# S5 scan over sixteen groups at a time, its matrices on VectorE alone, and the value projection moved ahead of queries and keys

## The chip, the cores and the metric

The kernel runs on one core of one Trainium2 chip. The metric is the device time of one execution in microseconds; below, the median of three executions is given, and beside it the time and the span of the one execution that was profiled. The engines are TensorE (PE), VectorE (DVE), ScalarE (ACT), GpSimd (POOL) and SyncE (SP), which here issues the transfers.

## The reference, cut to what matters

A two-layer trunk works on 1152 tokens of 1024 features (1024 latent tokens and 128 context tokens). The first layer runs neighbourhood attention and a bidirectional diagonal state-space model (S5) side by side on one input projection:

```
hp = h @ w_in
q, k, v, u = split(hp)             # 512 features each
q = rmsnorm(q); k = rmsnorm(k)
na = neighbourhood_attention(q, k, v)
# S5: 32 groups of 16 channels, 64 complex states, two directions
bu = B_bar u                       # per group
h[t] = A_bar * h[t-1] + bu[t]      # complex, forward and backward
y = gelu(D u + Re(C h))
y = y * sigmoid(y @ w_glu + b_glu)
out = concat(na, y) @ w_out
```

After it come a gated ConvFFN, a layer of grouped-query attention, and another ConvFFN. Nothing of those is touched here.

## The kernel before, in words

**The stage.** What matters lies in the first 510 us of some 3270. After the tables of S5 and the first part of the modulation are made, the 1152 tokens are normalised in six chunks of 192 (tiles `xc`, `n_t`, `n_rs`) and split into a high and a low part (`h0h` and `h0l`). A projection multiplies each by the split weights (`w_hi`, `w_lo`) in three products; DVE makes `h0l`, POOL makes `w_lo`. Then four blocks of `u` (tile `u_p`), eight blocks of queries and keys of three column chunks each (24 chunks; `qk_norm` takes the squares on ACT, a mean on PE into `ps_n`, two operations on `q_rs` and one on `qk_o` on DVE), and eighteen tiles of values (`v_o`). The accumulators `ps_b` have three buffers, so PE can be at most three chunks ahead of the operation that empties them.

**S5 setup.** `s5_setup` builds, for eight blocks of four groups each, input matrices (`s5tmp` into `s5win`, transposed on PE) and output matrices (`s5T`) with a product table (`s5tz`, many small matmuls). Of each block's twelve tensor operations six stood on DVE and six on POOL.

**S5 main.** `s5_main` handles the 32 groups in four parts of eight. `states` multiplies the inputs `s5U` by `s5win` on PE, ACT copies the result into `s5L`, and DVE scans it: time is cut in nine segments of sixteen steps, and all segments step at once, so that one step is four operations (two products `s5t`, two additions to `s5L`) on a strided slice; a short second scan (`s5hin`) joins the segments. `outputs` expands the segments' start states (`s5p`, four products of 128x512, and one sum), adds them to the scanned states (`s5hp`, two operations of 64x1016), multiplies on PE, stores `s5Y`, reloads it transposed (`s5yc`), applies gelu (`s5yo`) and stores it for the gate. In each block two of the four products and one of the two additions stood on POOL. `s5L` had two buffers, and the scan of one part was woven with the outputs of the part before.

**Order.** Instructions are placed on each engine's queue by a scheduler from the order of the program, the dependencies and the buffers; S5 is issued from within the projection's loops with high priority (`s5_on`). Every queue runs strictly in its order. After the stage, `mix` loads the four gelu results, the gate (`ygh`, `glu_ps`) needs all four, and the attention loads `na_q` and `na_k` from the stored queries and keys.

Of the kernel before, what the change touches and what calls it, by code (L numbers as in the profile page):

```python
# [29 lines left out]
BH = slice(64, 128)  # L30
# [130 lines left out]
def s5_setup(K, I, S, bp, P):  # L161
# [102 lines left out]
    for b in range(8):  # L264
        g = slice(4 * b, 4 * b + 4)
        d4 = lambda ap: ap.rearrange("p (g s c) -> p g s c", g=4, s=8)
        tmp = [d4(t) for t in half("X0") + half("X1")]
        vv = [d4(t) for t in half("X2")]
        e = (dve, pool)
        P4 = lambda t: [bc(x[:, g], (128, 4, 8, 16), 3) for x in t]  # L270
        C4 = lambda t: [bc(x[:, g], (128, 4, 8, 16), 2) for x in t]
        cmul(K, vv, P4(pv), C4(bb), tmp, e=e)
        win = bp.tile([128, 2, 4, 128], F32, tag="W", name="s5win")
        with K.tc.high_priority():
            for r in range(2):
# [33 lines left out]
        tz = bp.tile([128, 240], F32, tag="tz", name="s5tz")  # L309
        act.activation(tz, pz[:, :240], AF.Copy)  # L310
        K.stt(tz[:, 112:128], i16, dd[:, b : b + 1], pz[:, 112:128], ALU.mult, ALU.add)
        K.load(S.tz[4 * b : 4 * b + 4].rearrange("g c n -> (g c) n"), tz)
        yield


def s5_main(K, I, S, bp, P, yg):
# [2 lines left out]


    dve, act, pool = K.dve, K.act, K.pool
    G = 8

    def step(cur, prev, aR, aS, shape):
        x = ((1, 3), (3,)) if len(shape) == 4 else ((1,), ())
        for src, c in ((prev, bc(aR, shape, *x[0])), (prev[:, ::-1], bc(aS, shape, *x[1]))):
            t = bp.tile([128, 2, G, 9], F32, tag="t", name="s5t", bufs=2)
            if len(shape) == 3:
                t = t[:, :, :, 0]
            K.tt(t, src, c, ALU.mult)  # L330
            K.tt(cur, cur, t, ALU.add)

    def states(m, out):
        gs = slice(G * m, G * m + G)
        out.U = U = bp.tile([128, G, 144], F32, tag="U", name="s5U", bufs=2)
        K.load(U, S.ud[m].rearrange("s c g k -> (s c) g k"))
        out.L = L = bp.tile([128, 2, G, 144], F32, tag="L", name="s5L", bufs=2)
        out.hin = hin = bp.tile([128, 2, G, 8], F32, tag="hin", name="s5hin", bufs=2)
        for b2 in range(2):
            win = bp.tile([128, 2, 4, 128], F32, tag="W", name="s5win2", bufs=2)  # L340
            K.load(win.rearrange("p r g n -> p (r g n)"), S.win[2 * m + b2])
            for n0 in (0, 2):
                for r in range(2):
                    pt = P("s")
                    for j in range(2):
                        K.pe.matmul(pt[:, j * 144 : (j + 1) * 144], lhsT=win[:, r, n0 + j], rhs=U[:, 4 * b2 + n0 + j], start=True, stop=True)
                    src = pt[:, :288].rearrange("p (g n) -> p g n", n=144)
                    dst = L[:, r, 4 * b2 + n0 : 4 * b2 + n0 + 2]
                    act.activation(dst[FH], src[FH], AF.Copy)
                    act.activation(dst[BH, :, 0:128], src[BH, :, 127::-1], AF.Copy)  # L350
                    act.activation(dst[BH, :, 128:144], src[BH, :, 143:127:-1], AF.Copy)
                yield
        Lv = L.rearrange("p r g (s j) -> p r g s j", j=16)
        for j in range(1, 16):
            step(Lv[:, :, :, :, j], Lv[:, :, :, :, j - 1], S.a8R[:, gs], S.a8S[:, :, gs], (128, 2, G, 9))
            yield

        pool.tensor_copy(S.fin[:, :, gs], Lv[:, :, :, 8, 15])
        dve.tensor_copy(hin[:, :, :, 0], S.init[:, :, gs])
        for i in range(7):  # L360
            dve.tensor_copy(hin[:, :, :, i + 1], Lv[:, :, :, i, 15])
            step(hin[:, :, :, i + 1], hin[:, :, :, i], S.a128R[:, gs], S.a128S[:, :, gs], (128, 2, G))
        yield

    def outputs(m, q):
        wia = bp.tile([128, 8, 128], F32, tag="wia", name="s5wia")
        for s in range(8):
            K.load(wia[16 * s : 16 * s + 16], S.tz[8 * m : 8 * m + 8, 0:16, (7 - s) * 16 : (7 - s) * 16 + 128].rearrange("g c n -> c g n"))
        Y = bp.tile([128, G, 144], F32, tag="Y", name="s5Y")
        init = S.init[:, :, G * m : G * m + G]  # L370
        for b2 in range(2):
            lg = slice(4 * b2, 4 * b2 + 4)
            g = slice(G * m + 4 * b2, G * m + 4 * b2 + 4)
            wout = bp.tile([128, 2, 4, 128], F32, tag="V", name="s5wout")
            K.load(wout.rearrange("p r g n -> p (r g n)"), S.wout[2 * m + b2])
# [1 line left out]
            p = [bp.tile([128, 2, 4, 8, 16], F32, tag=f"P{i}", name=f"s5p{i}") for i in range(2)]  # L377
            for r in range(2):
                shp = (128, 4, 8, 16)
                K.tt(p[0][:, r], bc(q.hin[:, r, lg], shp, 3), bc(S.awR[:, g], shp, 2), ALU.mult)  # L380
# [4 lines left out]
            lb = q.L[:, :, lg]  # L385
# [9 lines left out]
            for n0, n1 in ((0, 2), (2, 4)):  # L395
                pt = P("s")
                for j in range(n0, n1):
                    K.acc(
                        pt[:, (j - n0) * 144 : (j - n0 + 1) * 144],
                        [(wia[:, b2 * 4 + j], q.U[:, b2 * 4 + j]), (wout[:, 0, j], hp[:, 0, j]), (wout[:, 1, j], hp[:, 1, j])],  # L400
                    )
                act.activation(Y[:, b2 * 4 + n0 : b2 * 4 + n1], pt[:, : (n1 - n0) * 144].rearrange("p (g n) -> p g n", n=144), AF.Copy)
            yield
# [10 lines left out]
    class Part:  # L414
        pass

    old = None
    for m in range(5):
        new = Part()
        todo = [states(m, new)] if m < 4 else []  # L420
        if old:
            todo.append(outputs(m - 1, old))
        while todo:
            for g in todo[:]:
                if next(g, g) is g:
                    todo.remove(g)
                else:
                    yield
        old = new

# [903 lines left out]
def tile_hybrid_step(ctx, tc, I, O):  # L1334
# [110 lines left out]
    for m in range(8):  # L1445
        u = W.get(I["w_qk"][m])
        for a, b in CH:
# [8 lines left out]
                K.load(O["na_k"][128 * (m - 4) : 128 * (m - 4) + 128], o[:, 256:384])  # L1456
            s5_on(3)
            next(parts, None)
    for hf in range(2):
        ws = [W.get(I["w_v0"][hf, kk]) for kk in range(2)]  # L1460
        for t in range(9):
            ps = P("b")
            token_major(K, ps[:, :256], ws, H, t)
            o = qp.tile([128, 384], F32, tag="qk", name="v_o", bufs=2)
            act.activation(o[:, :256], ps[:, :256], AF.Copy)
            K.load(S.vd[t][:, 256 * hf : 256 * hf + 256], o[:, :256])
            if t == 8:
                K.load(O["na_v"][:, 256 * hf : 256 * hf + 256], o[:, :256])
# [352 lines left out]
```

## Time and profile before

| quantity | value |
|---|---|
| median of 3 runs | 3267.01 us (3266.26 to 3275.08) |
| profiled execution: time, span | 3276.04 us, 3274.2 us |
| PE busy, share of the span | 2979.5 us, 91% |
| DVE busy | 1853.3 us, 57% |
| ACT busy | 1379.8 us, 42% |
| POOL busy | 1168.9 us, 36% |

The shares are averages over stages with different limits: over the whole span PE leads, but in the stage of this change other engines end the waits. A timeline row gives the start, the duration, the engine, the line, the operation, out<-in and the count of instructions merged into the row; a bracket at its end says how long the engine sat idle ahead and what ended it.

### The profile page before, as it was taken

How to read it: one execution, taken by the hardware profiler on the slowest of the kernel's cores; microseconds unless marked ns; L12 is line 12 of the kernel's file. 1: busy time of each engine (PE TensorE's matmuls, PEld its weight loads, DVE VectorE, ACT ScalarE, POOL GpSimd, SP SyncE). 2: the span in 40 equal slices, each digit the busy share in tenths (PEclk: the TensorE clock that was granted, in tenths of full speed). 3: DMA queues.
4: the chain of work that ended last, by engine and by line, in shares of the span. 5: the costliest groups of instructions: out<-in, count | busy, mean ns of one | idle time of the engine just before them, and what ended most of it. 6: DMA issues, size and time to landing. Idle time of an engine off the chain costs nothing.

```text
span 3274.2 us, 49873 instructions
## 1 busy us (share of the span) xinstructions
PE 2979.5 (91%) x19218; PEld 2619.3 (80%) x19218; DVE 1853.3 (57%) x3582; ACT 1379.8 (42%) x2650; POOL 1168.9 (36%) x827
## 2 busy tenths in 40 slices
PE   5899898996799999799998999999977999997999
PEld 2687786786799999688888954444767999997999
DVE  9868936646565565332245757675465655653330
ACT  2344436644444444333354345544344444443332
POOL 5522332232111111255554456767421111113554
PEclk8899999998899999899999999999988999998999
DMA  7656473111212222677644411110112122125653
GB/s 240 183 153 212 142 177 77 42 65 58 79 64 78 81 73 69 235 231 235 224 141 109 120 48 40 29 40 14 68 58 79 61 81 81 66 77 203 201 187 107
DMA packets 190495, 371.17 MB, mean 113 GB/s; under 512 B 35376, under 2 KB 104240, under 8 KB 189360
## 3 DMA queue, kind: packets, MB, share of 16 engines
q1 hardware_dynamic: 190000, 367.91, 35.9%
q8 instruction: 151, 2.47, 0.3%
q14 instruction: 88, 0.72, 0.1%
q0 software_dynamic: 256, 0.07, 0.0%
HBM read 287.41 MB, written 75.13 MB: 111 GB/s over the span
## 4 chain that ended last, share of the span: by engine, by line
PE 73%; DVE 14%; DMA 6%; ACT 2%; issue 2%; SPq 1%; POOL 1%; DVEq 0%; ACTq 0%; POOLq 0%
PE ps_u L1127 17%; PE ps_d L1317 16%; PE ps_b L68 12%; PE ps_w L1127 9%; PE ps_v L1127 4%; PE gq_ps L68 4%; PE gq_po L809 3%; PE na_po L590 1%; PE gq_m L724 1%; SPq L63 1%; DVE w_raw L74 1%; DMA ff_r<-d_f 1%; PE na_ps L68 1%; PE na_px L545 1%; DVE n_t L71 1%
## 5 line engine op out<-in xcount | busy, mean ns | idle before, releaser
L74 POOL TENSOR_TENSOR w_lo<-w_raw,w_hi 128x1024 fp32r<-128x1024 f32 x178 | 431.2, 2424 | 517.8 <-ACT w_hi L879 456.7
L1317 PE MATMUL ps_d<-ff_f,w_hi 128*128 128x384 f32 x2112 | 552.9, 341 | 42.1 <-DVE ff_g L74 37.3
L74 POOL TENSOR_TENSOR ff_w<-w_raw,ff_w 128x512 fp32r<-128x512 f32 x88 | 131.2, 1491 | 903.3 <-ACT ff_w L1115 903.3
L1317 PEld LDWEIGHTS ps_d<-ff_f,w_hi 128*128 128x128 f32 x2112 | 388.5, 191 | 66.9 <-DVE ff_g L74 38.3
L1127 PE MATMUL ps_u<-q_T,ff_w 128*128 128x288 f32 x2772 | 392.4, 296 | 7.7 <-ACT ff_p L1141 7.7
L1127 PEld LDWEIGHTS ps_u<-q_T,ff_w 128*128 128x128 f32 x2772 | 377.3, 189 | 8.7 <-ACT ff_p L1141 8.7
L1317 PE MATMUL ps_d<-ff_f,w_lo 128*128 128x384 f32 x1056 | 358.3, 339 | 1.6 <-POOL w_lo L74 1.5
L879 ACT ACTIVATE w_hi<-w_raw 128x1024 fp32r<-128x1024 f32 x178 | 187.7, 1056 | 343.9 <-PE ps_d L1317 222.1
L74 POOL TENSOR_TENSOR gq_acc<-gq_acc,gq_p 128x512 f32<-128x512 f32 x210 | 274.7, 1337 | 133.9 <-DVE gq_acc L74 95.1
L71 DVE SCALAR_TENSOR_TENSOR ff_g<-ff_G,pack,ff_g 128x127 f32<-128x127 f32 (+2 forms) x264 | 165.5, 641 | 193.1 <-ACT ff_g L1164 188.5
L1115 ACT ACTIVATE ff_w<-w_raw 128x512 fp32r<-128x512 f32 x264 | 164.4, 624 | 230.3 <-DVE w_raw L74 210.5
L825 ACT ACTIVATE gq_p<-gq_ps 128x512 f32<-128x512 f32 x288 | 157.5, 594 | 163.1 <-PE gq_ps L68 159.3
L726 DVE TENSOR_REDUCE gq_mx<-gq_m 128x1 f32<-128x384 f32 x336 | 164.7, 548 | 92.1 <-PE gq_m L724 91.9
L71 DVE SCALAR_TENSOR_TENSOR x<-ps_d,ada,x 128x384 f32<-128x384 f32 (+1 forms) x64 | 28.7, 509 | 315.0 <-PE ps_d L1317 315.0
L1317 PEld LDWEIGHTS ps_d<-ff_f,w_lo 128*128 128x128 f32 x1056 | 201.7, 191 | 5.7 <-issue 3.5
L1127 PE MATMUL ps_v<-q_B,ff_w 128*128 128x288 f32 x924 | 133.3, 299 | 62.6 <-ACT ff_w L1115 61.6
L74 DVE TENSOR_TENSOR ff_f<-ff_r,ff_f 128x384 fp32r<-128x384 f32 x130 | 124.3, 969 | 115.5 <-ACT ff_f L1290 114.4
L1127 PEld LDWEIGHTS ps_v<-q_B,ff_w 128*128 128x128 f32 x924 | 127.2, 191 | 64.9 <-ACT ff_w L1115 63.2
L68 PEld LDWEIGHTS gq_ps<-gq_qq,gq_kk 128*128 128x128 f32 x288 | 54.6, 190 | 135.5 <-ACT gq_p L825 89.1
L68 PE MATMUL ps_b<-mixh,w_hi 128*128 128x288 f32 x512 | 153.6, 302 | 6.9 <-DVE mix L74 6.4
L74 DVE TENSOR_TENSOR ff_w<-w_raw,ff_w 128x512 fp32r<-128x512 f32 x176 | 121.3, 689 | 67.1 <-ACT ff_w L1115 67.1
L809 PE MATMUL gq_po<-gq_p,gq_v 128*64 128x512 f32 x576 | 155.6, 619 | 0.0
(382 smaller groups left out, 6981.8 us busy)
## 6 DMA issues: line engine op xcount, KB each, us to landing
w_raw<-in_w_down_dram SPq DMA_DIRECT2D x132, 512.0 KB, 4.1
w_raw<-in_w_up_dram SPq DMA_DIRECT2D x88, 512.0 KB, 3.9
w_raw<-in_ada_w_dram SPq DMA_DIRECT2D x80, 512.0 KB, 5.3
d_f<-ff_g SPq DMA_DIRECT2D x44, 576.0 KB, 4.0
ff_r<-d_f SPq DMA_DIRECT2D x130, 192.0 KB, 3.6
w_raw<-in_w_qk_dram SPq DMA_DIRECT2D x18, 512.0 KB, 4.0
d_xs<-x SPq DMA_DIRECT2D x6, 1536.0 KB, 6.2
x<-d_xs SPq DMA_DIRECT2D x6, 1536.0 KB, 9.3
```

What stands on the lines that cost most here:

```text
L63: return self.nc.sync.dma_start(out=out, in_=in_)
L68: self.pe.matmul(ps, lhsT=l, rhs=r, start=i == 0, stop=i == n - 1)
L71: self.dve.scalar_tensor_tensor(out=out, in0=in0, scalar=scalar, in1=in1, op0=op0, op1=op1)
L74: (eng or self.dve).tensor_tensor(out=out, in0=a, in1=b, op=op)
L545: pe.transpose(px[:, (j - j0) * 128 : (j - j0 + 1) * 128], pb[:, j * 128 : (j + 1) * 128], K.ident)
L726: K.dve.tensor_reduce(out=mx[:, i, c : c + 1], in_=ps, axis=AX.X, op=ALU.max)
L809: pe.matmul(po[64 * p : 64 * p + 64], lhsT=v, rhs=pts[kt][p], start=kt == 0, stop=kt == 8)
L825: act.activation(e, ps, AF.Exp, scale=0.125)
L879: K.act.activation(hi, raw, AF.Copy)
L1115: K.act.activation(t[:, 0], src, AF.Copy)
L1127: self.K.pe.matmul(ps, lhsT=t[:, p, w], rhs=B(q, k), start=start and k == i == 0, stop=k == 3 and i == 2, skip_group_check=not start)
L1317: K.pe.matmul(ps[j], lhsT=wt[:, w], rhs=ft, start=f == 0 and q == 0, stop=f == NF - 1 and q == 2)
```

## The change

The scan takes two parts of sixteen groups (`GS`) in place of four of eight, so each scan instruction is twice as wide and there are half as many. `s5L` is one tile of sixteen groups with one buffer, and the work is no longer woven: states of the first half, outputs of its two parts, then the second half. The six operations of each setup block and the three of each output block that POOL ran go to DVE. The inputs `s5U` are loaded a second time for the outputs. The value projection moves from behind the queries and keys to ahead of them, and the setup's blocks are issued within it; `u_p` gets two buffers.

```diff
@@ s5_setup
-        e = (dve, pool)
-        cmul(K, vv, P4(pv), C4(bb), tmp, e=e)
+        cmul(K, vv, P4(pv), C4(bb), tmp)
...
-        K.tt(t9[1], pr, nci, ALU.mult, pool)
-        K.tt(T[:, 1], pi, cr, ALU.mult, pool)
-        K.tt(T[:, 1], t9[1], T[:, 1], ALU.subtract, pool)
+        K.tt(t9[1], pr, nci, ALU.mult)
+        K.tt(T[:, 1], pi, cr, ALU.mult)
+        K.tt(T[:, 1], t9[1], T[:, 1], ALU.subtract)
@@ s5_main
-    G = 8
+    G, GS = 8, 16
...
-            t = bp.tile([128, 2, G, 9], F32, tag="t", name="s5t", bufs=2)
+            t = bp.tile([128, 2, GS, 9], F32, tag="t", name="s5t", bufs=2)
...
-        out.L = L = bp.tile([128, 2, G, 144], F32, tag="L", name="s5L", bufs=2)
+        out.L = L = bp.tile([128, 2, GS, 144], F32, tag="L", name="s5L")
...
-                K.tt(p[1][:, r], bc(q.hin[:, 1 - r, lg], shp, 3), bc(S.awS[:, r, g], shp, 2), ALU.mult, pool)
+                K.tt(p[1][:, r], bc(q.hin[:, 1 - r, ls], shp, 3), bc(S.awS[:, r, g], shp, 2), ALU.mult)
...
-            K.tt(hp[BH, :, :, 126::-1], lb[BH, :, :, 0:127], pf[BH, :, :, 0:127], ALU.add, pool)
+            K.tt(hp[BH, :, :, 126::-1], lb[BH, :, :, 0:127], pf[BH, :, :, 0:127], ALU.add)
...
-    for m in range(5):
-        new = Part()
-        todo = [states(m, new)] if m < 4 else []
-        if old:
-            todo.append(outputs(m - 1, old))
...
+    for h in range(2):
+        part = Part()
+        yield from states(h, part)
+        for m in (2 * h, 2 * h + 1):
+            yield from outputs(m, part)
@@ tile_hybrid_step
-        up = qp.tile([128, 8, 144], F32, tag="up", name="u_p")
+        up = upool.tile([128, 8, 144], F32, tag="up", name="u_p", bufs=2)
...
-        for _ in range(2):
-            next(setup, None)
+    for hf in range(2):
+        ws = [W.get(I["w_v0"][hf, kk]) for kk in range(2)]
+        for t in range(9):
+            ps = P("b")
+            token_major(K, ps[:, :256], ws, H, t)
...
+            if t % 2 == 0:
+                next(setup, None)
...
-    for hf in range(2):
-        ws = [W.get(I["w_v0"][hf, kk]) for kk in range(2)]
...
-            s5_on(2)
```

What this does to the queues is shown at three places. The first is DVE's queue at the first setup blocks, ahead of the normalisation (`ada` and `A` are the modulation, `n_rs` the first chunk's root). Before:

```order
L74 TENSOR_TENSOR s5tmp<-s5tmp 128x512
L78 TENSOR_SCALAR SawS<-SawS 128x512
L74 TENSOR_TENSOR s5T<-s5tabs 128x576 x2
L74 TENSOR_TENSOR s5t_892<-s5tabs 128x576
L74 TENSOR_TENSOR s5T<-s5t_892,s5T 128x576
L74 TENSOR_TENSOR s5tmp<-s5tabs 128x512 x2
L74 TENSOR_TENSOR ada_74<-ps_a,pack 128x8 x4
```

After:

```order
L74 TENSOR_TENSOR s5tmp<-s5tabs 128x512 x2
L74 TENSOR_TENSOR s5tmp<-s5tmp 128x512
L78 TENSOR_SCALAR SawS<-SawS 128x512
L74 TENSOR_TENSOR s5T<-s5tabs 128x576 x4
L74 TENSOR_TENSOR s5tmp<-s5tmp 128x512
L74 TENSOR_TENSOR s5t_1215<-s5tabs 128x576
L74 TENSOR_TENSOR ada_74<-ps_a,pack 128x8 x4
L74 TENSOR_TENSOR s5t_1216<-s5tabs 128x576
L74 TENSOR_TENSOR s5T<-s5t_1215,s5T 128x576
```

The block's other six operations now stand in DVE's queue among the six it had; seven of the eight blocks still stand ahead of the last `h0l`, as before, and POOL's queue holds `w_lo` there and no setup product.

The second place is ACT's queue in the value projection. Before, the eighteen `v_o` copies came last, and only the last S5 outputs stood among them. Now it reads:

```order
L1437 ACTIVATE v_o<-ps_b 128x256 x8
L877 ACTIVATE w_hi<-w_raw 128x1024 x2
L1437 ACTIVATE v_o<-ps_b 128x256
L398 ACTIVATE s5hp<-s5L 64x8x15
L399 ACTIVATE s5hp<-s5L 64x8x15
L1437 ACTIVATE v_o<-ps_b 128x256 x7
L408 ACTIVATE s5Y<-ps_s 128x288
```

The two copies from the scanned `s5L` into `s5hp` stand behind the ninth value tile, so the tenth to the eighteenth queue behind the end of the first scan. On PE the first output block stands 27 matmuls ahead of the end of the values, and all `s5win` products of the first half stand ahead of the 34th value matmul.

The third place is SP's queue at the end of the stage. Before, the four `mix` loads stood among the value stores, and the attention's loads behind the last of them:

```order
L63 DMA d_yg<-s5yo 128x1152
L63 DMA w_raw<-in_w_out_dram 128x1024
L63 DMA d_vd<-v_o 128x256
L63 DMA mix<-d_yg 128x1152
L63 DMA d_vd<-v_o 128x256
L63 DMA mix<-d_yg 128x1152 x3
L63 DMA d_vd<-v_o 128x256 x6
```

After:

```order
L63 DMA d_yg<-s5yo 128x1152
L63 DMA d_qd<-qk_o 128x384 x2
L63 DMA out_na_k_dram<-qk_o 128x128
L63 DMA mix<-d_yg 128x1152 x4
L63 DMA na_q<-d_qd 64x1152 x2
L63 DMA na_k<-d_qd 64x1152
```

The `mix` loads and every load of the attention now stand behind the last gelu's store. In DVE's queue the second scan starts behind the norm of chunk 8; five norms (chunks 9 to 13) stand within it, two within the joining of its segments, four (16 to 19) among its output blocks, and five behind.

## Rows read from the trace of the kernel before

**Rows 1.** Windows, core 0: busy us (count) of each engine, PE clock, DMA share, GB/s

```profile
30.00:152.00 122.00, 84.12 (x722) 65.29 (x718) 121.25 (x198) 47.59 (x99) 81.04 (x51) 0.82 0.58 178
...
207.00:260.00 53.00, 47.59 (x270) 42.54 (x270) 49.57 (x125) 19.01 (x44) 16.71 (x17) 0.97 0.50 145
```

**Rows 2.** Timeline of DVE in the normalisation: start, us, engine, line, operation, shapes, count

```profile
56.45 8.14 DVE L71 SCALAR_TENSOR_TENSOR n_t<-xc,A,n_rs 128x192 f32<-128x192 f32 x8
...
75.20 2.71 DVE L71 SCALAR_TENSOR_TENSOR n_t<-xc,A,n_rs 128x192 f32<-128x192 f32 x8
...
151.37 0.54 DVE L71 SCALAR_TENSOR_TENSOR h0l<-n_t,ada,h0h 128x64 fp32r<-128x64 f32 x2
```

**Rows 3.** Timeline of POOL: a product of the setup, and a low part of weights

```profile
57.37 1.38 POOL L74 TENSOR_TENSOR s5tmp<-s5tmp 128x512 f32<-128x512 f32 x1
...
202.83 2.39 POOL L74 TENSOR_TENSOR w_lo<-w_raw,w_hi 128x1024 fp32r<-128x1024 f32 x1 [13.34 <-ACT w_hi L879]
```

**Rows 4.** Timeline of DVE in the first part's scan and joining

```profile
190.64 0.41 DVE L74 TENSOR_TENSOR s5t<-s5L,Sa8R 128x144 f32<-128x144 f32 x1 [26.07 <-ACT s5L L351]
...
191.28 0.85 DVE L74 TENSOR_TENSOR s5L<-s5L,s5t 128x144 f32<-128x144 f32 x2
192.17 0.40 DVE L74 TENSOR_TENSOR s5t<-s5L,Sa8R 128x144 f32<-128x144 f32 x1
...
202.88 2.53 DVE L74 TENSOR_TENSOR s5t<-s5L,Sa8R 128x144 f32<-128x144 f32 x1
...
216.73 0.19 DVE L74 TENSOR_TENSOR s5t<-s5hin,Sa128R 128x16 f32<-128x16 f32 x1
216.83 0.18 DVE L74 TENSOR_TENSOR s5t<-s5hin,Sa128S 128x16 f32<-128x16 f32 x1
...
217.41 0.19 DVE L74 TENSOR_TENSOR s5t<-s5hin,Sa128R 128x16 f32<-128x16 f32 x1
```

**Rows 5.** Timeline and groups of DVE: prices of the other operations

```profile
14.97 1.28 DVE L74 TENSOR_TENSOR s5tmp<-kr,s5tmp 128x512 f32<-128x512 f32 x2
...
348.29 1.21 DVE L74 TENSOR_TENSOR s5hp<-s5L,s5p 64x1016 f32<-64x1016 f32 x1
...
L71 DVE SCALAR_TENSOR_TENSOR qk_o<-ps_b,gains,q_rs 128x384 f32<-128x384 f32 x24 | 14.7, 612 | 0.1
```

**Rows 6.** Chain of work that ended last, in order: start, us, what, count

```profile
156.89 3.71 PE ps_b L68 x21
160.60 3.13 PE ps_s L68 x64
...
174.16 0.98 PE ps_s L346 x8
...
290.33 0.65 PE ps_n L1015 x2
...
452.26 5.94 PE ps_b L68 x48
```

**Rows 7.** Timelines of ACT and SP at the end, and DMA groups (KB, us to landing)

```profile
425.53 0.41 ACT L402 ACTIVATE s5Y<-ps_s 128x288 f32<-128x288 f32 x1 [0.81 <-PE ps_s L68]
...
435.96 2.62 ACT L410 ACTIVATE s5yo<-s5yc 128x1152 f32<-128x1152 f32 x1
...
459.39 2.21 ACT L1491 ACTIVATE ygh<-mix 128x1152 fp32r<-128x1152 f32 x2
...
460.86 1.13 SPq L63 DMA_DIRECT2D na_q<-d_qd  x2
...
d_yg<-s5yo SPq DMA_DIRECT2D x4, 576.0 KB, 3.2
...
mix<-d_yg SPq DMA_DIRECT2D x4, 576.0 KB, 7.4
```

**Rows 8.** Waits from 190 to 500 us: who for whom, us in total, times, longest

```profile
ACT v_o L1465 <- DMA d_vd<-v_o: 15.2, 5, 5.1
...
ACT L410 <- DMA s5yc<-d_yd: 13.4, 3, 5.8
```

More of the change, by code (lines that the diff above doesn't have):

```diff
@@ L331, in step, with inputs, states @@
             K.tt(cur, cur, t, ALU.add)
-    def states(m, out):
-        gs = slice(G * m, G * m + G)
-        out.U = U = bp.tile([128, G, 144], F32, tag="U", name="s5U", bufs=2)
+    def inputs(m):
+        U = bp.tile([128, G, 144], F32, tag="U", name="s5U", bufs=2)
         K.load(U, S.ud[m].rearrange("s c g k -> (s c) g k"))
-        out.L = L = bp.tile([128, 2, G, 144], F32, tag="L", name="s5L", bufs=2)
-        out.hin = hin = bp.tile([128, 2, G, 8], F32, tag="hin", name="s5hin", bufs=2)
-        for b2 in range(2):
+        return U
+    def states(h, out):
+        gs = slice(GS * h, GS * h + GS)
+        out.L = L = bp.tile([128, 2, GS, 144], F32, tag="L", name="s5L")
+        out.hin = hin = bp.tile([128, 2, GS, 8], F32, tag="hin", name="s5hin", bufs=2)
+        for b in range(4):
+            if b % 2 == 0:
+                U = inputs(2 * h + b // 2)
             win = bp.tile([128, 2, 4, 128], F32, tag="W", name="s5win2", bufs=2)
-            K.load(win.rearrange("p r g n -> p (r g n)"), S.win[2 * m + b2])
+            K.load(win.rearrange("p r g n -> p (r g n)"), S.win[4 * h + b])
             for n0 in (0, 2):
@@ L345, in states @@
                     for j in range(2):
-                        K.pe.matmul(pt[:, j * 144 : (j + 1) * 144], lhsT=win[:, r, n0 + j], rhs=U[:, 4 * b2 + n0 + j], start=True, stop=True)
+                        K.pe.matmul(pt[:, j * 144 : (j + 1) * 144], lhsT=win[:, r, n0 + j], rhs=U[:, 4 * (b % 2) + n0 + j], start=True, stop=True)
                     src = pt[:, :288].rearrange("p (g n) -> p g n", n=144)
-                    dst = L[:, r, 4 * b2 + n0 : 4 * b2 + n0 + 2]
+                    dst = L[:, r, 4 * b + n0 : 4 * b + n0 + 2]
                     act.activation(dst[FH], src[FH], AF.Copy)
@@ L354, in states @@
         for j in range(1, 16):
-            step(Lv[:, :, :, :, j], Lv[:, :, :, :, j - 1], S.a8R[:, gs], S.a8S[:, :, gs], (128, 2, G, 9))
+            step(Lv[:, :, :, :, j], Lv[:, :, :, :, j - 1], S.a8R[:, gs], S.a8S[:, :, gs], (128, 2, GS, 9))
             yield
@@ L361, in states @@
             dve.tensor_copy(hin[:, :, :, i + 1], Lv[:, :, :, i, 15])
-            step(hin[:, :, :, i + 1], hin[:, :, :, i], S.a128R[:, gs], S.a128S[:, :, gs], (128, 2, G))
+            step(hin[:, :, :, i + 1], hin[:, :, :, i], S.a128R[:, gs], S.a128S[:, :, gs], (128, 2, GS))
         yield
@@ L369, in outputs @@
         Y = bp.tile([128, G, 144], F32, tag="Y", name="s5Y")
+        U = inputs(m)
         init = S.init[:, :, G * m : G * m + G]
@@ L372, in outputs @@
             lg = slice(4 * b2, 4 * b2 + 4)
+            ls = slice(8 * (m % 2) + 4 * b2, 8 * (m % 2) + 4 * b2 + 4)
             g = slice(G * m + 4 * b2, G * m + 4 * b2 + 4)
@@ L379, in outputs @@
                 shp = (128, 4, 8, 16)
[L380 to L381 removed]
+                K.tt(p[0][:, r], bc(q.hin[:, r, ls], shp, 3), bc(S.awR[:, g], shp, 2), ALU.mult)
+                K.tt(p[1][:, r], bc(q.hin[:, 1 - r, ls], shp, 3), bc(S.awS[:, r, g], shp, 2), ALU.mult)
             K.tt(p[0], p[0], p[1], ALU.add)
@@ L384, in outputs @@
             pf = p[0].rearrange("p r g s j -> p r g (s j)")
-            lb = q.L[:, :, lg]
+            lb = q.L[:, :, ls]
             K.tt(hp[FH, :, :, 1:128], lb[FH, :, :, 0:127], pf[FH, :, :, 0:127], ALU.add)
-            K.tt(hp[BH, :, :, 126::-1], lb[BH, :, :, 0:127], pf[BH, :, :, 0:127], ALU.add, pool)
+            K.tt(hp[BH, :, :, 126::-1], lb[BH, :, :, 0:127], pf[BH, :, :, 0:127], ALU.add)
             pool.tensor_copy(hp[FH, :, :, 0], init[FH, :, lg])
@@ L399, in outputs @@
                         pt[:, (j - n0) * 144 : (j - n0 + 1) * 144],
-                        [(wia[:, b2 * 4 + j], q.U[:, b2 * 4 + j]), (wout[:, 0, j], hp[:, 0, j]), (wout[:, 1, j], hp[:, 1, j])],
+                        [(wia[:, b2 * 4 + j], U[:, b2 * 4 + j]), (wout[:, 0, j], hp[:, 0, j]), (wout[:, 1, j], hp[:, 1, j])],
                     )
@@ L415, in s5_main @@
         pass
-    old = None
-    for m in range(5):
-        new = Part()
-        todo = [states(m, new)] if m < 4 else []
-        if old:
-            todo.append(outputs(m - 1, old))
[L423 to L429, printed above, removed]
+    for h in range(2):
[3 more added lines that the diff above has]
+            yield from outputs(m, part)
 def na_attention(K, I, S, mix, psS, psT, psO):
@@ L1418, in tile_hybrid_step @@
     st.release()
-    qp = K.sb("proj0", 1, "right")
+    upool = K.sb("proj0u", 1, "right")
     for m in range(4):
         u = W.get(I["w_u"][m])
-        up = qp.tile([128, 8, 144], F32, tag="up", name="u_p")
+        up = upool.tile([128, 8, 144], F32, tag="up", name="u_p", bufs=2)
         for a, b in CH:
@@ L1430, in tile_hybrid_step @@
             K.load(S.ud[m].rearrange("s c g k -> g c s k")[g], up[16 * g : 16 * g + 16])
-        for _ in range(2):
-            next(setup, None)
+    upool.release()
+    qp = K.sb("proj0", 1, "right")
+    for hf in range(2):
[3 more added lines that the diff above has]
+            token_major(K, ps[:, :256], ws, H, t)
+            o = qp.tile([128, 384], F32, tag="qk", name="v_o", bufs=2)
+            act.activation(o[:, :256], ps[:, :256], AF.Copy)
+            K.load(S.vd[t][:, 256 * hf : 256 * hf + 256], o[:, :256])
+            if t == 8:
+                K.load(O["na_v"][:, 256 * hf : 256 * hf + 256], o[:, :256])
+            if t % 2 == 0:
+                next(setup, None)
     for _ in setup:
@@ L1458, in tile_hybrid_step @@
             next(parts, None)
-    for hf in range(2):
-        ws = [W.get(I["w_v0"][hf, kk]) for kk in range(2)]
[L1461 to L1468, printed above, removed]
-            s5_on(2)
     s5_on(1000)
```

## The prediction

> **What bounds the kernel now.** The table's shares say TensorE, 91% of the span; but a share over 3270 us says nothing of a stage of 510. I read windows first. From 30 to 152 us VectorE is busy 121.25 of 122 us and TensorE 84.12; in 207 to 260, where the second scan runs among the norms, 49.57 of 53 [rows 1]. So VectorE sets the pace where the change works. The chain of waits agrees in part: it runs on TensorE's accumulators between these places, 21 products of a projection taking 3.71 us (0.177 each), 64 of the table product 3.13, 8 state products 0.98 (0.1225 each), 48 value products 5.94 (0.124 each), the two of a mean 0.65 [rows 6].
>
> VectorE's busy time is not all work. Eight `n_t` take 2.71 us alone and 8.14 at 56 us [rows 2], while POOL runs a setup product of 1.38 us [rows 3]. A scan product takes 0.41 us, and 2.53 at 202.88, where POOL runs a `w_lo` of 2.39 us from 202.83 [rows 3, 4]. So I price an overlapping POOL operation at about its own length, and a `w_lo` at 2.53 − 0.41 = 2.1 us of VectorE.
>
> I set up the new times stage by stage, by the order of the queues shown above.
>
> **Up to the last `h0l` (before: 151.9 us [rows 2]).** The change puts 6 more setup operations of each block on VectorE and takes the stretching away. From 30 us: seven blocks of twelve, half 128x512 at 1.28/2 = 0.64 [rows 5], half 128x576 at 0.64·576/512 = 0.72, less about 0.05 of overlap each: 53. Five chunks, `n_t` and `h0l` at 2.71 each and three root operations of that width (2.71/8 each): 32. The last chunk, 32 narrow ones at 0.54/2 = 0.27 or a little more [rows 2]: 9. Small table operations: 4.5. Three `w_lo` at 2.1: 6.4. Sum 105, so 135, 17 us earlier. If the stretch stayed, 42 added operations at 0.68 would make it 29 later; from work without stretch alone (no `w_lo`), 23 earlier. I take 17: the stretched rows all have a POOL operation beside them.
>
> **To the first scan (before: 190.64 [rows 4]).** All states of the first half now stand ahead of it on TensorE: after the last `h0l` come 216 projection products (38.2), 64 state products (7.8), two table blocks (6.3), and 31 value products (3.8): 56 us, before ScalarE's last copy of about 1.5. It starts at 193, 2 later than before, though it covers twice the groups. The 17 us gained are spent here.
>
> **The wide step.** No row shows 128x288 on this strided layout. Products of 16 elements start 0.10 us apart (216.73 to 216.83 [rows 4]), of 144 elements 0.32 (the two ahead of 191.28 take 0.64 from 190.64): 1.72 ns an element, so 288 take 0.57. A step now takes 192.17 − 190.64 = 1.53 [rows 4], 4·0.32 and 0.25 of dependency; the wide one 4·0.57 + 0.25 = 2.53, against 2·1.53 = 3.06 for two parts. Lower end: by the slope to the 128x512 row ((0.64 − 0.10)/496 = 1.1 ns) 0.50, and 2.25 a step; upper end: no gain, 3.06. I take 2.53, the two rows on the same layout. Fifteen steps are 38 us (34 to 46), 8 less a half than now; with three `w_lo` (6.3) the first scan ends at 237.
>
> **TensorE beside it.** The values have moved here to cover the scan. ScalarE's two copies into `s5hp` wait for the scan's end with the tenth to eighteenth value tile behind them, so TensorE, three buffers ahead, stops after twelve tiles: 12·24 − 31 = 257 products of 0.124 are 32 us, then some of queries' and keys' means, until about 226; it idles 11 us to 237. Behind it stand 6 tiles (17.9), one output block (24·0.1225 = 2.9) and 12 projection products (2.1): 260. The segments' joining (7 rounds of 0.68, 216.73 to 217.41 [rows 4], with copies) and the first `s5p` and `s5hp` (four of 0.64 and two of 1.21 [rows 5]) end by 249 and are hidden by these tiles; if the idle time were not closed by then, at most 5 us would come on top.
>
> **To the second scan.** `s5L` has one buffer, so its states come behind the first half's outputs. TensorE: 180 projection products (31.9), 8 means (5.2), two output blocks (5.9), 64 states (7.8), some 58 small ones of the modulation priced as a state product (7): 58, so 318, and the scan begins at 319.5. VectorE has in that time 2 output blocks (12) and nine norms at about 1.5 (`qk_o` 0.61 [rows 5] and two operations of that width): 26 of 58, hidden.
>
> **The second half, on VectorE.** Scan 38, five norms within it 7.5, joining 5.3, two norms 3, four output blocks, each four of 0.64, a sum and two additions of 1.21, so 6.0 with overlap: 24, though two belong to the first half if they slip; four norms 6; four `w_lo` 8.4. Sum 92: 411.5. TensorE has 16 chunks of 24 products in the same stretch (68), means (10) and blocks (12): 90, equal within my error. From there a norm, 19 products and the last block to its `s5Y` copy: 418.5. Before, that copy ended at 425.94 [rows 7]. So 7 us of gain are left at this point.
>
> **The tail.** `mix` and the attention's loads stood among value stores and now stand behind the last gelu; the values that covered the last output's way are gone. From the copy's end to the last gelu's end are 435.96 + 2.62 − 425.94 = 12.6 us; then the store 3.2, four issues of `mix` of about 0.5, a landing 7.4 [rows 7]: 418.5 + 12.6 + 3.2 + 2 + 7.4 = 443.7 for `ygh`, which started at 459.39: 16 earlier. `na_q` would issue at 436.5, against 460.86 [rows 7]. TensorE idles some 20 us there, with nothing to cover it, but this idle time lies ahead of the earlier end and is in the sum. The second load of `s5U` lies beside the scan (no price found; if not hidden, at most a transfer of some 3 us, the store's size class).
>
> What comes behind, the gate and attention, is unchanged. Net −16. The profiled execution took 3276.04 us, 9.0 over the median of 3267.01; so 3276 − 16 = 3260 of its kind, and **3251** for a median.
>
> **A rule that speaks against it.** The Trainium skill ("Perfetto Trace Analysis", section "Optimizing Scalar/DVE Operations") says that where VectorE is saturated, moving some of its work to ScalarE or even GpSimd may make sense; this change moves work the other way, onto an engine busy 121 of 122 us. The same sentence adds that GpSimd and VectorE share a read port, so offloading between these two may not help; the stretched rows agree with the second half. By the first half alone the sum is that of rival three below.
>
> **Rivals.** *A cheap wide step:* 2.25 a step saves 4 us more in each half (8), `mix` lands in 5 rather than 7.4, and the three `w_lo` of the first stage fall where VectorE waits (6): 17 more, 3234. For it: the slope to 128x512; against: that row reads contiguous data. Chance 0.12.
>
> *The tail or a queue absorbs it:* the second scan starts at 319, while before, four parts were woven and spread; where the wide step costs 3.06 (8 more a half), or ScalarE's strict order delays the second half by 10 to 16, the net is −8 to +8: about 3267. For it: no row shows a cheaper wide step on this layout; in the stretch to 411 VectorE and TensorE are equal, so any miss adds. Chance 0.20.
>
> *ScalarE's waits go on the path, slower:* it waited 15.2 us for value stores and 13.4 for `s5yc` loads [rows 8], hidden now under the value projection's long work. With the last outputs at the stage's end both would lie on the path: −16 + 28.6 = +13, 3280. It decides where the second half's last block comes more than 16 us later than my 418.5. Against: value stores now lie early. Chance 0.09.
>
> *VectorE overloaded, slower:* should stretching stay, `h0l` comes 29 later instead of 17 earlier, the outputs add 16·0.64 + 8·1.21 = 20 to VectorE, and both scans give back 16: +33, 3300. Against: it needs POOL operations beside it that the order no longer has; in the stage's first part only three `w_lo` are left. Chance 0.04.
>
> **How the numbers follow.** My forecast, a gain of 8 to 30 us, has 0.55; that its lower end lies within what can be told from no change gives 0.07 of it to "same". About 0.3%, 10 us, is that bound. Faster: 0.48 + 0.12 = 0.60; same 0.07 + 0.20 = 0.27; slower 0.13. The range reaches from the cheap step with a little beyond, 3226, to the edge of the slower cases, 3278; the forecast's own range is 3237 to 3259.
>
> **What would show it.** Right: last `h0l` at about 135 and no `n_t` group over 3 us but beside a `w_lo`; 128x288 rows of 0.57 to 0.6 us apart and steps near 2.5; first scan from 193 to 237, with TensorE idle for ScalarE's `s5hp` copy behind it; second scan from about 319; last `s5Y` at 418, `ygh` at 444 and `na_q` issued at 437. Wrong: `h0l` not earlier (the stretch is not POOL's); TensorE waiting at the first `s5hp` beyond 251; the second scan later than 330, or a tail longer than 25 us from the last `s5Y` to `ygh`, which would leave nothing of the gain.

## The result, and the profile after

The changed kernel is slower, by less than 1% but clear of the noise: a median of 3296.78 us against 3271.05 of the kernel before beside it, a ratio of 1.0075 with a 95% interval of 1.0052 to 1.0098. The profiled execution took 3291.99 us, 16 more than that of before; its span is 3290.2.

Windows of the changed kernel, core 0: busy us (count) of PE, PEld, DVE, ACT and POOL, then PE clock, DMA share and GB/s. The first and the third row stand against [rows 1]; the two rows of the kernel before that belong to the fourth and the last follow in a fence of their own.

```profile
30.00:152.00 122.00, 85.95 (x787) 79.61 (x786) 111.11 (x253) 49.97 (x105) 14.87 (x4) 0.82 0.50 150
152.00:207.00 55.00, 55.00 (x378) 55.00 (x377) 10.44 (x17) 22.67 (x64) 7.77 (x7) 1.00 0.65 191
207.00:260.00 53.00, 42.56 (x341) 41.37 (x340) 51.56 (x98) 8.81 (x21) 7.55 (x7) 0.90 0.23 75
260.00:320.00 60.00, 55.69 (x323) 43.41 (x321) 20.36 (x25) 27.47 (x52) 10.21 (x15) 1.00 0.83 246
...
420.00:470.00 50.00, 39.22 (x212) 34.92 (x211) 25.19 (x35) 22.82 (x36) 9.42 (x15) 0.90 0.52 152
470.00:510.00 40.00, 21.53 (x142) 20.52 (x143) 18.58 (x22) 16.29 (x23) 7.16 (x12) 0.75 0.94 207
```

The kernel before:

```profile
260.00:320.00 60.00, 55.11 (x312) 42.91 (x311) 55.42 (x138) 26.28 (x57) 15.77 (x16) 0.97 0.62 195
...
470.00:510.00 40.00, 26.98 (x180) 25.27 (x181) 29.67 (x44) 22.02 (x43) 16.52 (x14) 0.85 0.77 152
```

VectorE runs more operations from 30 to 152 us (253, before 198), is busy for less time, and finishes the normalisation early, as forecast. The row to look at is the fourth: from 260 to 320 us VectorE is busy for 20.36 of 60 us, between the outputs of the first half and the scan of the second. Before, this engine was busy for 55.42 of these 60 us. The other one is the last: TensorE is busy for 21.53 of 40 us, before for 26.98, and its granted clock is 0.75 of full speed in the mean of this stretch, before 0.85.

The timeline of VectorE in the changed kernel shows the steps that were forecast ([rows 2, 4] show those of before):

```profile
86.11 2.70 DVE L71 SCALAR_TENSOR_TENSOR n_t<-xc,A,n_rs 128x192 f32<-128x192 f32 x8
...
131.80 3.55 DVE L71 SCALAR_TENSOR_TENSOR h0l<-n_t,ada,h0h 128x128 fp32r<-128x128 f32 x15
...
196.29 0.67 DVE L74 TENSOR_TENSOR s5t<-s5L,Sa8R 128x288 f32<-128x288 f32 x1 [45.29 <-ACT s5L L355]
196.87 0.66 DVE L74 TENSOR_TENSOR s5t<-s5L,Sa8S 128x288 f32<-128x288 f32 x1
...
198.89 0.66 DVE L74 TENSOR_TENSOR s5t<-s5L,Sa8R 128x288 f32<-128x288 f32 x1
...
248.44 2.44 DVE L74 TENSOR_TENSOR s5hp<-s5L,s5p 64x1016 f32<-64x1016 f32 x2
...
343.46 0.66 DVE L74 TENSOR_TENSOR s5t<-s5L,Sa8R 128x288 f32<-128x288 f32 x1 [2.69 <-ACT s5L L355]
...
361.67 2.71 DVE L74 TENSOR_TENSOR s5t<-s5L,Sa8S 128x288 f32<-128x288 f32 x1
```

The last `h0l` ends at 131.80 + 3.55 = 135.35; an `n_t` group is 2.70 again; the first scan starts at 196.29, its products stand 0.58 apart and a step lasts 2.60. All that is near the forecast. The product of 2.71 us stands beside a `w_lo` that POOL runs from 361.16 for 2.80 us. The second scan starts at 343.46; the forecast had 319.5.

ScalarE's timeline in the changed kernel, against [rows 7]; the bracket gives the idle time ahead and its releaser:

```profile
218.39 0.36 ACT L1437 ACTIVATE v_o<-ps_b 128x256 f32<-128x256 f32 x1
236.25 0.30 ACT L398 ACTIVATE s5hp<-s5L 64x120 f32<-64x120 f32 x1 [17.50 <-DVE s5L L74]
...
317.19 2.38 ACT L416 ACTIVATE s5yo<-s5yc 128x1152 f32<-128x1152 f32 x1
...
425.27 0.41 ACT L408 ACTIVATE s5Y<-ps_s 128x288 f32<-128x288 f32 x1
...
441.80 2.43 ACT L416 ACTIVATE s5yo<-s5yc 128x1152 f32<-128x1152 f32 x1
...
447.05 0.71 ACT L408 ACTIVATE s5Y<-ps_s 128x288 f32<-128x288 f32 x2 [1.19 <-DMA d_yg<-s5yo]
...
455.61 0.41 ACT L408 ACTIVATE s5Y<-ps_s 128x288 f32<-128x288 f32 x1 [4.90 <-PE ps_s L68]
457.08 0.41 ACT L408 ACTIVATE s5Y<-ps_s 128x288 f32<-128x288 f32 x1 [1.06 <-PE ps_s L68]
...
467.47 2.26 ACT L416 ACTIVATE s5yo<-s5yc 128x1152 f32<-128x1152 f32 x1
...
484.56 2.22 ACT L1490 ACTIVATE ygh<-mix 128x1152 fp32r<-128x1152 f32 x2 [12.38 <-DMA mix<-d_yg]
```

The last `s5Y` copy is at 457.08 (before: 425.53), and `ygh` starts at 484.56 (before: 459.39, [rows 7]): 25 us later. The medians differ by 26, but the two profiled executions by 16 only: that of the kernel before is 5 us over its median and that of the changed kernel 5 under. What lies behind `ygh`, which the change does not touch, took 9 us less in the latter.

### The profile page after: what moved, and what is told of

It reads as the page before. It is cut to its first block, busy times and chain, and to the rows that moved or that the text cites. A ratio compares the mean times of both kernels' runs of the same rounds, so it can differ in the third digit from the quotient of the medians.

```text
span 3290.2 us, 49668 instructions
## 1 busy us (share of the span) xinstructions
PE 2976.7 (90%) x19218; PEld 2617.4 (80%) x19218; DVE 1819.2 (55%) x3462; ACT 1380.1 (42%) x2651; POOL 1059.5 (32%) x753
## 4 chain that ended last, share of the span: by engine, by line
PE 73%; DVE 11%; DMA 6%; ACT 3%; issue 2%; SPq 1%; POOL 1%; ACTq 0%; DVEq 0%; POOLq 0%
PE ps_u L1125 17%; PE ps_d L1315 16%; PE ps_b L68 12%; PE ps_w L1125 8%; PE ps_v L1125 4%; PE gq_ps L68 4%; PE gq_po L807 3%; PE na_po L588 1%; DVE w_raw L74 1%; PE gq_m L722 1%; DMA gq_q<-d_qd 1%; SPq L63 1%; PE na_ps L68 1%; DMA ff_r<-d_f 1%; PE na_px L543 1%
```

## The experiments

Every ratio is to the kernel before on the same chip, with its 95% interval.

**The values put back behind queries and keys.** The changed kernel with

```
             K.load(S.ud[m].rearrange("s c g k -> g c s k")[g], up[16 * g : 16 * g + 16])
+        for _ in range(2):
+            next(setup, None)
...
-    for hf in range(2):
-        ws = [W.get(I["w_v0"][hf, kk]) for kk in range(2)]
...
-            if t % 2 == 0:
-                next(setup, None)
...
+    for hf in range(2):
+        ws = [W.get(I["w_v0"][hf, kk]) for kk in range(2)]
...
+            s5_on(2)
     s5_on(1000)
```

> The changed kernel with the value projection put back behind queries and keys (the setup blocks back among the u blocks), all else as changed. Theory one, the order of the projections costs the time: S5's last outputs, the gate's loads and the attention's loads no longer lie beside the values, and SyncE's queue stands still behind value stores during the first scan; then this kernel hides S5's end again and shows VectorE's 17 us of the norm stage: 10 to 20 us under the kernel before, some 3251 to 3261. Theory two, the halves of sixteen groups with one buffer and no weaving cost the time: S5's chain stays long, and this kernel is 10 to 25 us over the kernel before.

Measured: 1.0066 (1.0048 to 1.0084), 3296.05 us. Theory one falls. ScalarE's timeline of this run has `ygh` at the same time as the changed kernel, though the last value copy was at 456.05:

```profile
472.01 2.27 ACT L416 ACTIVATE s5yo<-s5yc 128x1152 f32<-128x1152 f32 x1 [8.82 <-DMA s5yc<-d_yd]
...
484.56 2.22 ACT L1491 ACTIVATE ygh<-mix 128x1152 fp32r<-128x1152 f32 x2 [10.28 <-DMA mix<-d_yg]
```

With values last too, S5 ends behind them, and `ygh` waits for the load of its last gelu. So S5's own chain sets the end, wherever the values stand. The time lies 22 us over the kernel before, as theory two had it.

**The halves alone.** The same, with the setup's and the outputs' operations given back to POOL:

```
-        cmul(K, vv, P4(pv), C4(bb), tmp)
+        cmul(K, vv, P4(pv), C4(bb), tmp, e=(dve, pool))
...
-            K.tt(hp[BH, :, :, 126::-1], lb[BH, :, :, 0:127], pf[BH, :, :, 0:127], ALU.add)
+            K.tt(hp[BH, :, :, 126::-1], lb[BH, :, :, 0:127], pf[BH, :, :, 0:127], ALU.add, pool)
```

> The kernel before with the halves of sixteen groups alone (one s5L buffer, no weaving, inputs loaded twice); values last and POOL's share of the matrices as before. Theory one: S5 has some 30 us of slack ahead of the end of the values, so within 6 us of the kernel before, 3265 to 3277. Theory two: 10 to 25 us over the kernel before.

Measured: 1.0104 (1.0091 to 1.0117), 3308.29 us, 34 over the kernel before and above the range of either theory. The halves cost more than the whole change; beside them the two moves to VectorE gain some 12 us (1.0104 to 1.0066). This kernel also keeps the two buffers of `u_p`; they are in the kernel of early values below too, which costs nothing.

**Each move to VectorE alone**, in the kernel before:

```
-        cmul(K, vv, P4(pv), C4(bb), tmp, e=e)
+        cmul(K, vv, P4(pv), C4(bb), tmp)
...
-        K.tt(T[:, 1], pi, cr, ALU.mult, pool)
+        K.tt(T[:, 1], pi, cr, ALU.mult)
```

> The kernel before with the six setup operations of each block moved from POOL to VectorE, nothing else. Both theories: the last h0l at about 135 in place of 152, the first scan 17 us earlier, and 10 to 17 us under the kernel before, 3254 to 3261. A third theory, that VectorE pays for them in full, gives 15 to 29 us over it.

Measured: 0.9994 (0.9985 to 1.0002): no change that can be told, and none of the three theories. The last `h0l` ends some 6 us earlier (145.88), not 17, and the first scan starts at 189.14. VectorE is busy for less time, as forecast (109.07 us against 121.25), but in the old order it now waits, longest 5.4 us for a store of `s5T`. The windows of this run show why so little arrives: from 152 us TensorE has no idle time, as before the change, so only what it did more ahead of 152 (87.33 us against 84.12 in [rows 1]) can come back.

```profile
30.00:152.00 122.00, 87.33 (x705) 68.47 (x702) 109.07 (x246) 48.87 (x101) 11.55 (x4) 0.80 0.59 183
152.00:207.00 55.00, 55.00 (x408) 54.45 (x406) 18.64 (x48) 21.27 (x59) 11.04 (x8) 1.00 0.68 183
```

And the outputs:

```
-                K.tt(p[1][:, r], bc(q.hin[:, 1 - r, lg], shp, 3), bc(S.awS[:, r, g], shp, 2), ALU.mult, pool)
+                K.tt(p[1][:, r], bc(q.hin[:, 1 - r, lg], shp, 3), bc(S.awS[:, r, g], shp, 2), ALU.mult)
...
-            K.tt(hp[BH, :, :, 126::-1], lb[BH, :, :, 0:127], pf[BH, :, :, 0:127], ALU.add, pool)
+            K.tt(hp[BH, :, :, 126::-1], lb[BH, :, :, 0:127], pf[BH, :, :, 0:127], ALU.add)
```

> The kernel before with the three output operations of each block moved from POOL to VectorE, nothing else. Stretched VectorE rows beside POOL's products shrink by about what the moved operations add (20 us over eight blocks): within 6 us of the kernel before. The third theory: 10 to 20 us over it, since VectorE is busy nearly throughout from 207 to 420.

Measured: 0.9972 (0.9962 to 0.9982), 3265.23 us: faster than expected. Run again later, beside two others:

> The kernel before with the outputs' move alone, once more on this chip, to stand beside the two others: 0.997 of the kernel before, as first measured; 0.999 or more would say that the first measurement was of its chip.

Measured: 0.9981 (0.9971 to 0.9990), 3263.58 us. This is the fastest kernel of the study, and the last `s5Y` copy starts at 415.21 in the first of the two runs, 10 us ahead of before. The rows of VectorE's output products (shortest, median and longest in ns; the first row is of the kernel before) show what changed:

```profile
L74 DVE TENSOR_TENSOR s5p<-s5hin,SawR x16: 678/1541/2853, 222.0 to 415.5; 128x512 f32<-128x512 f32 x16
```

```profile
L74 DVE TENSOR_TENSOR s5p<-s5hin,SawR x16: 677/686/693, 223.1 to 407.0; 128x512 f32<-128x512 f32 x16
```

Beside POOL's product one took 1.54 us in the median, without it 0.69, so four in a row take no longer than two pairs did. The two additions of a block, side by side at 2.58 (VectorE) and 2.88 us (POOL) before, take 1.21 each.

**Both moves**, the two edits above together in the kernel before.

> The kernel before with both moves to VectorE, the setup's six operations and the outputs' three; four parts woven and values last as before. If the two moves add up as measured apart (0.9994 and 0.9972 of the kernel before), 9 to 12 us under it, ratio 0.9965. If VectorE becomes too full with both, about level with it.

Measured: 0.9991 (0.9981 to 1.0002), 3269.26 us. The moves don't add up, and the second of the two expectations holds; the setup's gives nothing here beside the outputs'.

**Early values, but four woven parts.** The changed kernel with the parts, the buffers, the inputs and the loop of the kernel before in `s5_main`:

```
-    G, GS = 8, 16
+    G = 8
...
+            todo.append(outputs(m - 1, old))
+        while todo:
+            for g in todo[:]:
```

> Both moves to VectorE and the values ahead of queries and keys, but four woven parts of eight groups: the changed kernel without its wide halves. Theory two (the halves cost the time, the projections' order costs next to nothing): within 5 us of the kernel with the two moves alone, so under the kernel before. Theory one (the order costs it): 10 to 20 us over the kernel before, as with the changed kernel, since nothing of TensorE covers the last outputs.

Measured: 0.9984 (0.9974 to 0.9995), 3268.4 us. The projections' order alone costs nothing that can be told: beside it, both moves in the old order gave 0.9991. Against the changed kernel only the halves differ, and they cost 30 us (0.9984 to 1.0075). Its windows show VectorE fed in the stretch where it starved in the changed kernel:

```profile
260.00:320.00 60.00, 51.99 (x287) 38.63 (x288) 49.42 (x127) 25.32 (x53) 8.24 (x12) 0.94 0.58 187
```

**Four parts, not woven.** The kernel with both moves and

```
-            todo.append(outputs(m - 1, old))
-        while todo:
...
+    for m in range(4):
+        part = Part()
+        yield from states(m, part)
+        yield from outputs(m, part)
```

> The kernel with the two moves, four parts of eight groups, but each part's outputs ended before the next part's states are issued in the program; two s5L buffers. If the weaving of one part's scan with the outputs before it is what the halves lost, 15 to 35 us over the kernel with the two moves. If the one s5L buffer is what they lost, within 6 us of it, since the queues' order may still place the next states early.

Measured: 1.0146 (1.0133 to 1.0159), 3320.35 us, 51 over the woven kernel with both moves (3269.26) and more than the 15 to 35 expected, though `s5L` keeps two buffers and the scan its old width. The timeline of VectorE has the first products of the first and the fourth scan, and ScalarE's the last gelu and the gate; the second fence has the same two scans of the woven kernel with both moves:

```profile
188.95 0.40 DVE L74 TENSOR_TENSOR s5t<-s5L,Sa8R 128x144 f32<-128x144 f32 x1 [27.39 <-ACT s5L L350]
...
439.05 0.40 DVE L74 TENSOR_TENSOR s5t<-s5L,Sa8R 128x144 f32<-128x144 f32 x1 [27.46 <-ACT s5L L350]
```

```profile
187.12 0.40 DVE L74 TENSOR_TENSOR s5t<-s5L,Sa8R 128x144 f32<-128x144 f32 x1 [27.38 <-ACT s5L L350]
...
354.20 0.40 DVE L74 TENSOR_TENSOR s5t<-s5L,Sa8R 128x144 f32<-128x144 f32 x1 [1.54 <-ACT s5L L350]
```

```profile
497.36 2.26 ACT L409 ACTIVATE s5yo<-s5yc 128x1152 f32<-128x1152 f32 x1 [8.76 <-DMA s5yc<-d_yd]
511.59 2.22 ACT L1481 ACTIVATE ygh<-mix 128x1152 fp32r<-128x1152 f32 x2 [11.97 <-DMA mix<-d_yg]
```

From first to fourth scan are 250 us, 83 a part; in the woven kernel with both moves the first products stand at 187.12 and 354.20, 56 a part. So weaving is worth some 50 us of the kernel's time; the fourth scan itself starts 85 us later, but in the woven kernel S5 ends well ahead of the gate (last gelu to `ygh` 31 us, here 12), and that slack takes part of the rest. The kernel with halves, both moves and late values (1.0066) is 24 to 26 us better than this one. It has a wider step and one turn from outputs to states in place of three, and with them one `s5L` buffer and a second load. By the steps' prices the width is worth an estimated 14 us ((2·1.53 − 2.60)·15·2, from [rows 4] and the 2.60 above); no run tells the rest apart.

**Inputs kept, not loaded again.** The changed kernel with

```
-        U = bp.tile([128, G, 144], F32, tag="U", name="s5U", bufs=2)
+        U = bp.tile([128, G, 144], F32, tag="U", name="s5U", bufs=3)
...
-        U = inputs(m)
+        U = q.U[m % 2]
```

> The changed kernel with three buffers of inputs, kept through the outputs and not loaded again. If the second half's states start late because their inputs stand in SyncE's queue behind the store of a gelu (issued at 320 us) and wait for a buffer, the second scan starts 10 to 20 us ahead of 343 and the kernel is 8 to 20 us under the changed one. If TensorE's own order (its work of some 72 us between 260 and 342) sets that start, within 5 us of the changed kernel.

Measured: 1.0038 (1.0025 to 1.0050), 3283.94 us. The second scan starts at 337.03, 6 us earlier, between the two expectations; the whole gains some 12, as the first one had it. SyncE's timeline in the changed kernel shows what this took away: the inputs of the second half's second part stood behind a gelu's store.

```profile
319.60 0.33 SPq L63 DMA_DIRECT2D d_yg<-s5yo  x1
320.02 0.38 SPq L63 DMA_DIRECT2D s5U<-d_ud  x1
```

**The first half's gelus behind the second half's states**, on top of that:

```
+    def gate(m):
         yc = bp.tile([128, G, 144], F32, tag="yc", name="s5yc")
...
         yield from states(h, part)
+        if h:
+            for m in (0, 1):
+                yield from gate(m)
         for m in (2 * h, 2 * h + 1):
             yield from outputs(m, part)
+            if h:
+                yield from gate(m)
```

> The changed kernel with three input buffers kept (as in the earlier run) and with the first half's two gelus issued behind the second half's states in the program; in TensorE's queue 23 projection products and 4 modulation products fewer then stand ahead of the last state. If S5's one chain through the two halves sets the end of the stage, the second scan starts 5 to 12 us ahead of the 337 us of the run with kept inputs, and the kernel is 3 to 10 us under that run, ratio to the kernel before about 1.001 to 1.003. If something behind S5 (the gate's or the attention's loads) sets it, level with that run, 1.004.

Measured: 1.0031 (1.0017 to 1.0044), 3281.46 us, level with the run before it; the second scan starts at 338.99. That start didn't move, so this run doesn't say what an earlier one would bring. TensorE was busy for 94.5 us of 240 to 340 in it: with fewer products ahead of the states it waited elsewhere, longest 4.4 us for ScalarE's `w_hi`. The edit did not do what it was for: the two gelus ran at 298.78 and 312.38, still among the states, whose products stand from 291.7 to 336.6.

**Half of the values early, half late**, four woven parts, both moves. The kernel of early values with

```
-    for hf in range(2):
+    def values(hf, go):
         ws = [W.get(I["w_v0"][hf, kk]) for kk in range(2)]
...
+    values(0, lambda t: next(setup, None))
...
+    values(1, lambda t: s5_on(2))
     s5_on(1000)
```

> Four woven parts, both moves to VectorE, the first half of the values ahead of queries and keys and the second half behind them. The first half covers the first scan's start, the second the last gelu and the attention's loads, so 6 to 14 us under the kernel before if TensorE's idle time at 470 to 510 us is that of loads; if TensorE is the bound in all these orders, level with the kernel of four parts and early values, ratio 0.998 to 1.000.

Measured: 1.0003 (0.9991 to 1.0014), level and no gain of 6 to 14 us. And with the setup's operations back on POOL, as in the kernel before:

> The same with the setup's six operations on POOL as before and only the outputs on VectorE. If the setup's move gains nothing (TensorE has no idle time from 152 to 207 us in any run), within 4 us of the kernel with both moves; if the stretched norms cost, 5 to 15 us over it.

Measured: 1.0048 (1.0033 to 1.0063), 3287.07 us. Here the setup's move is worth 14 us, as the second expectation had it, and the window says where: with POOL at the setup, TensorE gets 72.85 us done ahead of 152, against 87.29 with VectorE alone in the same order.

```profile
30.00:152.00 122.00, 72.85 (x644) 63.28 (x643) 119.48 (x196) 46.46 (x96) 76.96 (x51) 0.76 0.42 130
```

## Why the prediction was wrong

**The normalisation: right.** 135 forecast, 135.35 measured. The stretch of VectorE's operations was POOL's: with it gone, no group of eight `n_t` takes over 2.71 us, and a wide scan product beside a `w_lo` still takes 2.71 instead of 0.65. So VectorE could take twelve operations a block and be busy for 111.11 us in place of 121.25. With the moves but the old order the last `h0l` came at 145.88, so the 17 us need the changed order too. The passage of the Trainium skill that the prediction names ("Perfetto Trace Analysis", section "Optimizing Scalar/DVE Operations") holds in its second half, that offloading between GpSimd and VectorE may not help: work moved off POOL cost VectorE nothing in this stage. Its first half would have given the case of an overloaded VectorE, which is the prediction's fourth rival and not, as it says there, the third.

**The first scan: right.** Start 193 forecast, 196.29 measured; a product 0.57 and 0.58, a step 2.53 and 2.60, the end 237 and 238.7, with two groups stretched by a `w_lo` where three were counted. TensorE's stop behind ScalarE's `s5hp` copies was to be 11 us; the waits of the trace show 10.4 (ScalarE itself waited 17.50 there). The third window's DMA share of 0.23 is beside it: SyncE issued nothing from 223 to 237.30, where its next entry was a value store, and the loads came later, at a share of 0.83.

**To the second scan: the step that failed.** The prediction priced it as TensorE's work, 58 us from 260, and started the scan at 319.5; it took 82, and the scan started at 343.46, 24 later. The groups of TensorE by line in the changed kernel, 260 to 342 us (busy us, mean ns | idle before, releaser), hold most of it; groups overlap, so their busy times add up to more than 82:

```profile
L68 PE MATMUL ps_b<-h0h,w_hi 128*128 128x384 f32 x72 | 26.8, 373 | 0.2 <-ACT w_hi L877 0.2
L68 PE MATMUL ps_b<-h0h,w_lo 128*128 128x384 f32 x71 | 25.4, 358 | 0.0
L68 PE MATMUL ps_b<-h0l,w_hi 128*128 128x384 f32 x72 | 25.4, 353 | 0.0
L916 PE MATMUL ps_a<-w_raw,cond 128*2 128x512 f32 x58 | 13.2, 622 | 0.8 <-DMA w_raw<-in_ada_w_dram 0.8
L350 PE MATMUL ps_s<-s5U,s5win 128*128 128x144 f32 x64 | 10.7, 292 | 3.7 <-ACT s5L L355 3.7
...
L1013 PE MATMUL ps_n<-q_sq,mean 128*128 128x384 f32 x16 | 6.7, 499 | 1.9 <-ACT q_sq L1011 1.9
```

There were 215 projection products, not 180, which is 6 us at 0.177, and counted from start to start they took 0.206 each, another 6; the modulation's 58 took 12.4 us so counted, not 7, since a 128x512 product is no state product; the outputs' part is 2 us more and the means 2 less. TensorE was busy for 75.3 of the 82. The rest are waits, the largest of 3.7 us for ScalarE's `s5L` copy, with the gelu of 317.19 just ahead of it in that queue: the rival on ScalarE's order in small. The second load of `s5U`, "at most a transfer of some 3 us" in the prediction, was too small as well: without it the second scan came 6 us earlier and the kernel gained some 12.

**What the change cost, by the runs.** The sum does follow the halves as a chain in series, so the loss of the weaving is in it; it came out too small by the sizes above and below. What the weaving was worth it never asked: it lists VectorE's 26 us of work in this stretch as hidden beside TensorE, but not what VectorE did there before. In the woven order one part's scan ran beside the outputs of the part ahead; in the halves nothing was scanned between a half's outputs and the next states. Four unwoven parts with unchanged width and buffers show this loss by itself: 51 us over three turns. The halves are 26 better (1.0146 to 1.0066). From the kernel before to the changed one, each step the ratio of two neighbours (0.1% is 3.3 us): the moves −3 us, the unweaving +51, the halves in place of four parts −26, the values' order +3 (1.0066 to 1.0075, inside the intervals). Such a row of steps makes the measured 25 of itself; what is shown by an edit alone is the 51, and the 30 between early values with four woven parts and the changed kernel.

**The second half: 99 us forecast, 114 measured** (343.46 to the copy's end at 457.49). It was summed as VectorE's work, 92 us, and that held: the last `s5hp` ends at 437.86, 94.4 after the scan's start.

```profile
435.43 2.43 DVE L74 TENSOR_TENSOR s5hp<-s5L,s5p 64x1016 f32<-64x1016 f32 x2 [1.79 <-PE ps_s L68]
```

What failed is the last block's way from there to its `s5Y` copy: 7 us forecast, 19.6 measured. ScalarE's timeline shows the larger part: from the `s5Y` copy at 425.27 to that at 447.05 lies the first part's whole way through store, reload and gelu, since `s5Y` and `s5yo` share one buffer. Behind it the last block's two copies still waited 4.90 and 1.06 us for TensorE. With four woven parts this way lay beside the next scan.

**The tail: nearly right.** From the end of the last `s5Y` copy to `ygh` 25 us forecast, 27.1 measured. But that "this idle time lies ahead of the earlier end" fell with the earlier end. At `ygh` the miss is 41 us, 484.56 against 443.7: 24 to the second scan, 2 of VectorE's work, 13 in the last block's way and 2 in the tail. Two of the prediction's own signs of being wrong came true, the second scan later than 330 and a tail of over 25 us.

**The rivals.** The one on ScalarE's waits set its point at a last block 16 us behind 418.5, and 3280. The block came 38.6 behind and the time was 3297: right in sign and place, but the cause was S5's chain, of which ScalarE's waits are a part. The one on an overloaded VectorE was wrong; this engine idled. That the change puts S5's chain itself at the end of the stage had no rival of its own.

**Still open.** What exactly holds the second scan back to 337 to 343 us is not settled: keeping the inputs moved it by 6, a change of ScalarE's and TensorE's order by nothing. The trace of the changed kernel narrows it: the 64 state products stand on TensorE from 297.3 to 341.8 us, though they are busy for 10.7, with projection and modulation products between them; in the run with kept inputs they stand from 295.6 to 335.8. No run placed them together. Why a projection product took 0.206 us here and 0.177 in [rows 6] is open too. A wide scan that is woven as well was not run; it would need a second `s5L` of 18 KB a partition.

## What to carry to other kernels

Before a wider instruction or a simpler order is priced, write down what each engine did in the gaps of a chain before, and who fills them after: here unweaving four parts cost 51 us of overlap, and the halves gave back 26. A gain upstream is worth only what the next saturated engine can take up: `h0l` came earlier and TensorE, with next to no idle time from 152 to 207, passed on almost none of it in one order and 14 us in another. Where halves or buffers make a chain serial, add its latencies (store, reload, gelu, copies in strict order) rather than the busy time of its busiest engine.

## What was unexpected of the hardware

Nothing of the chip itself contradicted the rows of before. Two prices were only seen here: a 128x288 scan product on the strided layout starts 0.58 us ahead of the next one (0.32 for 128x144), and TensorE's granted clock in 470 to 510 us, a mean over the stretch, was 0.75 in the changed kernel, where TensorE was busy for 21.53 of 40 us, 0.85 in the kernel before with 26.98, and 0.63 in the kernel of unwoven parts with 7.59. In the kernel of the halves alone it was 0.63 as well, with 16.02, so the busy time alone does not order these.
